# Four pairs of weight-word buffers and a separate half bank for one product in five sigmoid-gated head pairs of a hybrid attention block

## The chip, the cores and the metric

The kernel runs on one core of a Trainium2 chip. The metric is the device time of one execution in microseconds (us). Three runs of the kernel before gave 827.22, 828.13 and 829.1 us; the median is 828.13 us.

## What is computed

The reference is one decoder block on 512 tokens of width 2048: a normalisation, one large projection, two groups of attention heads, a gate on each head, an output projection, a residual and a final normalisation. Cut to what matters here:

```python
h = _rmsnorm(x, norm_g[l])
proj = h @ w_in[l]
(qa, kca, vca, ksa, vsa, kwa, vwa, za, ga, qb, kb, vb, zb) = jnp.split(proj, offsets, axis=-1)
...
y_a = o_a.reshape(B, S, WIDTH_A) * jax.nn.silu(za)
qb = _rope(_heads(qb, N_HEADS_B, HEAD_DIM_B))...
o_b = _banded_attention(qb, _rope(kb), vb, WIN_B, sink=sinks)
y_b = o_b.reshape(B, S, WIDTH_B) * jax.nn.silu(zb)
x = x + jnp.concatenate([y_a, y_b], axis=-1) @ w_out[l]
return _rmsnorm(x, final_g)
```

The change lies in the second group (`qb`, `zb`, `o_b`): 16 heads of 64 columns, handled as eight pairs of heads, each with 128 query columns and 128 gate columns to project.

## The kernel before, in words

Every float32 operand of a product is held as two words, a high word (`hi`, a rounded copy) and a low word (`lo`, the rest), and a product is three matmuls per block: high by high, high by low, low by high (`mm3`, lines 126 to 129, so the three lines L127, L128, L129 of the profile). For weights, ScalarE (ACT) makes the high word from the loaded block `raw` (tile `whi`, L643) and VectorE (DVE) subtracts it from `raw` to make the low word (`wlo`, L644); both are 128x1024. A pair `whi`, `wlo` is called words here. `words` (line 86) takes them from the pool `wp`, which has three buffers of each.

One head pair is projected by `pair(h)` (lines 689 to 770). The query and the gate columns together are a 2 by 2 block product, done with seven products instead of eight (the Winograd form of Strassen's scheme). Each has 8 blocks, so 24 matmuls of 128x256. Their names in the code and in this text are 22, p, 21, 12, w, u and q. Two PSUM banks hold them: `pa` and `pb`, from the pool `psp` (tile `pj`), which has two buffers; each bank has a left half H0 and a right half H1 of 256 columns.

- 22 goes to `pb` H0; ACT copies it, negated, to the tile `dd` (L732). 21 is added on top in the same place; ACT copies the sum to the right half of `zr` (L738).
- p goes to `pa` H0; DVE adds it to `dd` (L703, the helper `plus`). 12 is added on top in the same place; ACT copies the sum p+12 to the left half of the tile `t1` (`qv` in the code, L747).
- w goes to `pa` H1, and DVE adds it to `dd`. That is the last reader of `pa`.
- u goes to `pb` H1, q is added on top, and DVE adds them into the query and the gate.

Since `psp` has two buffers, the bank of `pa` becomes the `pb` of the next pair, so product 22 of pair h+1 can start when the last reader of `pa` of pair h is done. From h = 10 on (`wide`) a fifth load (`sm`, the sum of two quarters, added by an accumulating DMA that GpSimd issues, L699) takes the place of one addition on DVE.

The attention of the head pair before runs as jobs between these matmuls: scores (`spb`, L900 and L901, 16 matmuls), a masked maximum on DVE (`ttb`, L904), exponentials and scalings on ACT (L912, L918), transposes (`tp`, L930), words of the probabilities (`ph` on ACT L535, `pl` on DVE L536), products with the values (`opb`, L936, L937, L942), and a sum of two halves (`ob`: ACT L949, then DVE L950).

The order of the instructions on each engine is not written out by hand. A scheduler orders them when the program is built, by dependencies, by when buffers come free, and by times that it assumes; then each engine runs its list strictly in order. So a change in buffers reorders everything behind it. Loads go by the queue of SyncE (SP).

Pairs are counted here by h, 8 to 14; the third to the seventh pair of the group are 10 to 14. After pair 14 comes `plain(15, 0)`, the query columns of the last head pair as a plain product, whose first matmul takes the place of the next pair's 22.

Of the kernel before, what the change touches and what calls it, by code (L numbers as in the profile page):

```python
# [10 lines left out]
F32 = mybir.dt.float32  # L11
F32R = mybir.dt.float32r
AF = mybir.ActivationFunctionType
ALU = mybir.AluOpType
# [3 lines left out]
P = 128  # L18
S = 512
# [16 lines left out]
def hybrid_block(ctx, tc, xT, xtm, w0, w1s, w2s, wz, wq, wkb, wo0, wos, cw1, cw2, cpos, rope, tabs, sinks, gT, fg, out):  # L36
    nc = tc.nc
    pe, act, dve, pool = nc.tensor, nc.scalar, nc.vector, nc.gpsimd

    def sb(name, bufs=1, side=None):  # L40
        return tc.tile_pool(name=name, bufs=bufs, side=side)
# [40 lines left out]
    def raw():  # L82
        raws[0] += 1
        return weights(f"raw{raws[0] % 3}")

    def words(place):
        return [wp.tile([P, 1088], F32R, name=nm, tag=nm)[:, place:place + 1024] for nm in ("whi", "wlo")]

    def load_unit(src, width, rawp=None, opening=False, place=EVEN):
# [192 lines left out]
    H0, H1 = slice(0, 256), slice(256, 512)  # L282
# [246 lines left out]
    wk = wks.enter_context(sb("wk", bufs=2))  # L529
# [128 lines left out]
    def unit(raw):  # L658
        hi, lo = words(STILL)
        split(hi, lo, raw)  # L660
        return hi, lo
# [6 lines left out]
    def prod(bank, u, op, new, hooks=None):  # L668
        for m in range(8):
            cs = slice(m * P, m * P + P)  # L670
            ah, al = xf[op, m]
            mm3(bank, u[0][:, cs], u[1][:, cs], ah, al, new and m == 0, m == 7, not new)
            if m == 3:
                behind_mm((hooks or {}).get(op, ()))

    def swap_x(source):
        for part in range(2):
            ms = slice(4 * part, 4 * part + 4)
            for e in range(2):
                nc.sync.dma_start(even[e][:, ms], source[e, :, ms])  # L680
# [8 lines left out]
    def pair(h, early=(), hooks=None):  # L689
        src = wq[h - FIRST]  # L690
        early = list(early)
        wide = h > 9

        def load(tag, quarter, other=None):
            if early:
                return early.pop(0)
            t = load_quarter(src, tag, quarter)
            if other is not None:
                pool.dma_start(t, src[other], accum_op=ALU.add)  # L699
            return t  # L700

        def plus(out, a, b, op=ALU.add):
            return dve.tensor_tensor(out=out, in0=a, in1=b, op=op).ins  # L703

        if wide:
            c1, c2, c5, c3, c4 = tags
            tags[:] = c4, c1, c2, c3, c5
        else:
            c1, c2, c4, c3 = tags
            tags[:] = (c4, c1, c3, c2) if h < 9 else (c4, c1, "raw4", c3, c2)  # L710
        pa, pb = [psp.tile([P, S], F32, name="pj", tag="pj") for e in range(2)]

        qv = wk.tile([P, S], F32, name="t1", tag="t1", bufs=1)
        zr = wk.tile([P, S], F32, name="zr", tag="xr", bufs=1)
        d, jj = qv[:, H1], zr[:, H0]
        if wide:
            d = wb.tile([P, 256], F32, name="dd", tag="dd")
        x1 = load(c1, 3)
        u0 = unit(x1)
        x2 = load(c2, 0)  # L720
        u3 = unit(x2)
        if wide:
            sm = load(c5, 0, 2)
        else:
            sm = x2
            x4 = load(c4, 2)
            with ExitStack() as behind:
                if "jj" in last:
                    behind.enter_context(tc.issue_after(last["jj"]))
                plus(x2, x2, x4)  # L730
        prod(pb[:, H0], u0, "22", True, hooks)
        act.activation(d, pb[:, H0], AF.Copy, scale=-1.0)  # L732
        x3 = load(c3, 1)
        prod(pa[:, H0], u3, "p", True, hooks)
        plus(d, d, pa[:, H0])
        u2 = unit(x3)
        prod(pb[:, H0], u2, "21", False, hooks)
        act.activation(zr[:, H1], pb[:, H0], AF.Copy)  # L738
        plus(jj, d, zr[:, H1])
        u4 = unit(sm)  # L740
        if wide:
            x4 = load(c4, 2, 3)
        else:
            plus(x4, x4, x1)
        plus(sm, sm, x1)
        prod(pa[:, H0], u4, "12", False, hooks)
        act.activation(qv[:, H0], pa[:, H0], AF.Copy)  # L747
        plus(jj, jj, qv[:, H0], ALU.subtract)
        u1 = unit(x4)
        prod(pa[:, H1], u1, "w", True, hooks)  # L750
        plus(d, d, pa[:, H1])
        u5 = unit(sm)
        plus(sm, sm, x3)
        prod(pb[:, H1], u5, "u", True, hooks)
        plus(qv[:, H1], d, pb[:, H1])
        t2 = wk.tile([P, S], F32, name="t2", tag="t2", bufs=1)
        for a, b in ((0, 64), (64, 0)):
            dve.tensor_tensor(out=t2[a:a + 64], in0=qv[b:b + 64], in1=sinA[b:b + 64], op=ALU.mult)
        dve.tensor_tensor(out=qv, in0=qv, in1=cosA, op=ALU.mult)
        (pool if h < 8 else dve).tensor_tensor(out=qv, in0=qv, in1=t2, op=ALU.add)  # L760
        qq = q_split(qv) if h < 8 else qb_split(qv)
        u6 = unit(sm)
        prod(pb[:, H1], u6, "q", False, hooks)
        plus(jj, jj, pb[:, H1])
        behind_mm((hooks or {}).get("end", ()))
        last["jj"] = plus(zr, zr, rstdb, ALU.mult)
        st = wk.tile([P, S], F32, name="st", tag="st")
        act.activation(st, zr, AF.Tanh, scale=0.5)
        dve.scalar_tensor_tensor(out=st, in0=st, scalar=1.0, in1=zr, op0=ALU.add, op1=ALU.mult)
        return qq, st  # L770

    def plain(h, e, hooks=None):
        ps = psp.tile([P, S], F32, name="pj", tag="pj")
# [74 lines left out]
    wb = wbs.enter_context(sb("wb"))  # L848
# [4 lines left out]
    vb3 = wb.tile([P, P], F32, name="vb3")  # L853
    wb.tile([P, 3, 2, 2], F32, name="sums", tag="sums", bufs=2)
    wb.tile([P, 2, 256], F32, name="ttb", tag="ttb", bufs=4)
    wb.tile([P, S], F32, name="ob", tag="ob")
    nc.sync.dma_start(sk[:, 0, :], sinks)
    pool.tensor_scalar(sk[:, 1, :], sk[:, 0, :], -1.0, None, op0=ALU.mult)
    nc.sync.dma_start(cosB, ropeb[0])
# [22 lines left out]
    def attention(i, q2):  # L882
# [60 lines left out]

        def end():
            op = box["op"]
            ob = wb.tile([P, S], F32, name="ob", tag="ob")
            for v in range(2):
                hs = slice(v * 64, v * 64 + 64)
                act.activation(ob[hs], op[64:128, v, :], AF.Copy)  # L949
                dve.tensor_tensor(out=ob[hs], in0=op[0:64, v, :], in1=ob[hs], op=ALU.add)  # L950
            finish(8 + i, ob, box["st"])
# [6 lines left out]
    for i in range(7):  # L958
        hooks = {}
        if held:  # L960
            j, end, _ = held
            hooks = {"12": [j["s0"]], "w": [j["s1"]], "u": [j["k0"]], "q": [j["k2"], j["k3"]], "end": [j["k1"], end]}
        q2, st = pair(8 + i, (), hooks)
        if i == 0:
            back_b(0)
        if i == 2:
            back_b(1)
        held = attention(i, q2)
        held[2]["st"] = st
    swap_x(xd)  # L970
    for m in range(4):
        y_tile(m)
# [192 lines left out]
    for n in range(1, 4):  # L1165
# [55 lines left out]
        def plus(out, a, b, op=ALU.add):  # L1221
            dve.tensor_tensor(out=out, in0=a, in1=b, op=op)
# [12 lines left out]
        if n < 3:  # L1235
# [3 lines left out]
            jj = scratch()  # L1239
# [33 lines left out]
        else:  # L1273
# [64 lines left out]
            u1 = [pair()]  # L1338
# [121 lines left out]
```

## Time and profile before

| | |
|---|---|
| median of three runs | 828.13 us |
| the profiled execution, its own time | 826.69 us |
| its span, first to last instruction | 824.9 us |
| outside the span | 1.79 us |
| granted TensorE clock | 0.999 |
| pairs 10 to 14, about | 484 to 612 us of the span |

Times in the views are microseconds from the span's start. PE is TensorE, PEld its weight load. In a timeline row stand the start, the duration, the engine, the line, the output and inputs, and in brackets the idle time of that engine before it with what ended it. Names are without buffer numbers, so `pj` is `pa` or `pb` of any pair. A PE row of a 128x256 matmul lasts 0.28 us though the next starts about 0.12 us later, since matmuls overlap.

### The profile page before, as it was taken

The numbers are of one execution on the slowest core, as the hardware profiler recorded it, in microseconds if no ns is written. First come the engines' busy times: TensorE is split into PE (matmuls) and PEld (weight loads), VectorE is DVE, ScalarE is ACT, GpSimd is POOL, SyncE is SP. The second block draws the span as 40 slices with busy tenths as digits, with TensorE's granted clock in tenths as the row PEclk, the third lists the DMA queues.
The fourth block names the chain that finished last, engine by engine and source line by source line (L and its number), as shares of the span: only waits on it lengthen the run. The fifth ranks groups of instructions, "written<-read, shape, count | busy, mean of one in ns | idle before, by whom it ended". The sixth has DMA issues, their size and how long they took to land.

```text
span 824.9 us, 15435 instructions
## 1 busy us (share of the span) xinstructions
PE 797.2 (97%) x5782; PEld 750.0 (91%) x5782; DVE 685.4 (83%) x1271; ACT 529.4 (64%) x1103; POOL 76.4 (9%) x69
## 2 busy tenths in 40 slices
PE   9999999999999999999999989999999999999996
PEld 8788898988999999999999989989888788999996
DVE  7869786865898989998898789989977588977895
ACT  6734456662677867868776568766866776553545
POOL 4500002012011011011010000000000000000000
PEclk9999999999999999999999999999999999999999
DMA  9655886899712314412321685656595336597835
GB/s 320 206 200 166 290 301 195 272 333 353 223 52 66 104 40 141 154 51 79 116 78 63 195 206 135 186 145 166 139 314 183 91 102 218 138 302 181 259 79 204
DMA packets 60954, 145.29 MB, mean 176 GB/s; under 512 B 6352, under 2 KB 19920, under 8 KB 60880
## 3 DMA queue, kind: packets, MB, share of 16 engines
q1 hardware_dynamic: 57424, 132.26, 48.7%
q0 software_dynamic: 3168, 11.54, 8.1%
q8 instruction: 45, 0.74, 0.4%
q10 hardware_dynamic: 288, 0.52, 0.2%
q14 instruction: 29, 0.24, 0.1%
HBM read 121.65 MB, written 20.55 MB: 172 GB/s over the span
## 4 chain that ended last, share of the span: by engine, by line
PE 75%; DVE 9%; ACT 6%; DMA 5%; issue 3%; POOL 1%; SPq 0%; DVEq 0%; ACTq 0%
PE pj L127 13%; PE pj L129 13%; PE pj L128 13%; PE oa L128 4%; PE oa L129 4%; PE oa L127 4%; PE bank L129 4%; PE bank L127 4%; PE bank L128 3%; PE sp L567 3%; DVE wlo L644 2%; DMA raw<-wq 2%; ACT whi L643 1%; DVE raw L703 1%; DMA xr<-xT 1%
## 5 line engine op out<-in xcount | busy, mean ns | idle before, releaser
L127 PE MATMUL pj<-xh,whi 128*128 128x256 f32 (+1 forms) x560 | 170.7, 305 | 8.7 <-DVE sums L907 2.6
L129 PE MATMUL pj<-xh,wlo 128*128 128x256 f32 (+1 forms) x560 | 170.1, 304 | 1.7 <-DVE wlo L644 1.7
L128 PE MATMUL pj<-xl,whi 128*128 128x256 f32 (+1 forms) x560 | 168.8, 301 | 0.0
L643 ACT ACTIVATE whi<-raw 128x1024 fp32r<-128x1024 f32 x98 | 103.0, 1054 | 55.3 <-PE pj L128 33.2
L644 DVE TENSOR_TENSOR wlo<-raw,whi 128x1024 fp32r<-128x1024 f32 x98 | 121.4, 1242 | 12.7 <-ACT whi L643 12.3
L127 PEld LDWEIGHTS pj<-xh,whi 128*128 128x128 f32 x560 | 105.4, 188 | 15.8 <-ACT whi L643 3.0
L129 PEld LDWEIGHTS pj<-xh,wlo 128*128 128x128 f32 x560 | 105.6, 189 | 7.0 <-DVE wlo L644 2.5
L128 PEld LDWEIGHTS pj<-xl,whi 128*128 128x128 f32 x560 | 105.4, 188 | 4.2
L97 DVE TENSOR_TENSOR wlo<-raw,whi 128x512 fp32r<-128x512 f32 (+2 forms) x74 | 81.3, 1104 | 33.5 <-ACT whi L96 33.0
L96 ACT ACTIVATE whi<-raw 128x1024 fp32r<-128x1024 f32 (+1 forms) x73 | 65.5, 901 | 53.1 <-PE pj L128 17.3
L127 PE MATMUL pj<-pu,whi 128*128 128x256 f32 x224 | 64.2, 287 | 2.9 <-DVE sums L908 1.5
L129 PE MATMUL pj<-pu,wlo 128*128 128x256 f32 x224 | 63.2, 282 | 0.5 <-DVE wlo L644 0.5
L128 PE MATMUL pj<-pu,whi 128*128 128x256 f32 x224 | 63.3, 283 | 0.0
L703 DVE TENSOR_TENSOR raw<-raw 128x1024 f32<-128x1024 f32 x46 | 59.1, 1285 | 0.2
L128 PE MATMUL oa<-wlo,xh 128*128 128x256 f32 (+1 forms) x168 | 50.9, 303 | 0.7 <-DVE wlo L1008 0.7
L127 PE MATMUL oa<-whi,xh 128*128 128x256 f32 (+1 forms) x168 | 50.4, 303 | 1.0 <-DVE sums L904 1.0
L129 PE MATMUL oa<-whi,xl 128*128 128x256 f32 (+1 forms) x168 | 50.3, 302 | 0.0
L127 PEld LDWEIGHTS pj<-pu,whi 128*128 128x128 f32 x224 | 42.3, 189 | 4.2 <-issue 1.6
L129 PEld LDWEIGHTS pj<-pu,wlo 128*128 128x128 f32 x224 | 42.3, 189 | 1.0 <-DVE wlo L644 0.9
L128 PEld LDWEIGHTS pj<-pu,whi 128*128 128x128 f32 x224 | 42.2, 188 | 0.0
L536 DVE TENSOR_TENSOR pl<-tp,ph 128x512 fp32r<-128x512 f32 x56 | 37.7, 683 | 4.9 <-ACT ph L535 4.8
L535 ACT ACTIVATE ph<-tp 128x512 fp32r<-128x512 f32 x56 | 32.1, 588 | 12.4 <-PE tp L930 8.4
(372 smaller groups left out, 2325.6 us busy)
## 6 DMA issues: line engine op xcount, KB each, us to landing
raw<-wq SPq DMA_DIRECT2D x65, 512.0 KB, 4.1
raw<-cw SPq DMA_DIRECT2D x16, 512.0 KB, 5.2
raw<-wos SPq DMA_DIRECT2D x15, 512.0 KB, 5.0
raw<-wq POOLq DMA_DIRECT2D x10, 512.0 KB, 5.5
rw<-wos SPq DMA_DIRECT2D x10, 512.0 KB, 5.2
xr<-xT SPq DMA_DIRECT2D x16, 256.0 KB, 5.1
raw<-w SPq DMA_DIRECT2D x8, 512.0 KB, 4.4
fd<-ft SPq DMA_DIRECT2D x4, 1024.0 KB, 6.0
```

The costliest lines, as they stand in the source:

```text
L96: last["hi"] = act.activation(hi[:, :width], rw[:, :width], AF.Copy).ins
L97: last["lo"] = dve.tensor_tensor(out=lo[:, :width], in0=rw[:, :width], in1=hi[:, :width].bitcast(F32), op=ALU.subtract).ins
L127: pe.matmul(ps, ah, bh, start=first, stop=False, skip_group_check=go_on)
L128: pe.matmul(ps, ah, bl, start=False, stop=False, skip_group_check=go_on)
L129: recent["mm"] = pe.matmul(ps, al, bh, start=False, stop=last, skip_group_check=go_on).ins
L535: act.activation(ph, tp, AF.Copy)
L536: dve.tensor_tensor(out=pl, in0=tp, in1=ph.bitcast(F32), op=ALU.subtract)
L567: pe.matmul(sp[:, a:b], qq[:, qs], kk[0][:, ko:ko + b - a], start=pi == 0, stop=pi == 2)
L643: act.activation(hi, src, AF.Copy)
L644: last["lo"] = dve.tensor_tensor(out=lo, in0=src, in1=hi.bitcast(F32), op=ALU.subtract).ins
L703: return dve.tensor_tensor(out=out, in0=a, in1=b, op=op).ins
```

## The change

- From h = 10 on, a pool `w4` holds one more pair of word buffers, and every fourth call of `words` takes it. The pool is closed behind the last pair.
- From h = 10 on (`own`), product 12 does not go on top of p. ACT copies p alone (the copy L747 of before now reads p), 12 starts new in `pa` H1, and DVE takes it from there into the gate (`jj`) and onto the copy of p. Product w goes to `pa` H0. DVE adds p to `dd` from the copy in SBUF. That is one DVE operation of 128x256 more for each pair.
- To make room, `dd` takes the place of `pcr`, which the first group used, and `ob` shares the buffers of `pl`.

```diff
+    fourth = {"of": 0, "on": False}
     def words(place):
+        if fourth["on"]:
+            fourth["of"] += 1
+            if fourth["of"] % 4 == 0:
+                return [fourth["pool"].tile([P, 1024], F32R, name=nm, tag=nm) for nm in ("whi4", "wlo4")]
         return [wp.tile([P, 1088], F32R, name=nm, tag=nm)[:, place:place + 1024] for nm in ("whi", "wlo")]
...
         wide = h > 9
+        if h == 10:
+            fourth["pool"] = w4s.enter_context(sb("w4"))
+            fourth["pool"].tile([P, 48], F32, name="space")
+            fourth["on"] = True
...
-            d = wb.tile([P, 256], F32, name="dd", tag="dd")
+            d = wk.tile([P, 256], F32, name="dd", tag="pcr", bufs=1)
...
         prod(pa[:, H0], u3, "p", True, hooks)
-        plus(d, d, pa[:, H0])
+        own = wide
+        if own:
+            act.activation(qv[:, H0], pa[:, H0], AF.Copy)
+        else:
+            plus(d, d, pa[:, H0])
...
-        prod(pa[:, H0], u4, "12", False, hooks)
-        act.activation(qv[:, H0], pa[:, H0], AF.Copy)
-        plus(jj, jj, qv[:, H0], ALU.subtract)
+        if own:
+            prod(pa[:, H1], u4, "12", True, hooks)
+            plus(d, d, qv[:, H0])
+        else:
+            prod(pa[:, H0], u4, "12", False, hooks)
+            act.activation(qv[:, H0], pa[:, H0], AF.Copy)
+            plus(jj, jj, qv[:, H0], ALU.subtract)
         u1 = unit(x4)
-        prod(pa[:, H1], u1, "w", True, hooks)
-        plus(d, d, pa[:, H1])
+        if own:
+            plus(jj, jj, pa[:, H1], ALU.subtract)
+            plus(qv[:, H0], qv[:, H0], pa[:, H1])
+        w = pa[:, H0 if own else H1]
+        prod(w, u1, "w", True, hooks)
         u5 = unit(sm)
+        plus(d, d, w)
...
-            ob = wb.tile([P, S], F32, name="ob", tag="ob")
+            ob = wk.tile([P, S], F32, name="ob", tag="pl")
...
+    fourth["on"] = False
+    w4s.close()
```

Lines of the changed kernel are numbered higher: L644 of before is L650, L643 is L649, L703 is L713, L732 is L742, L738 is L752, L904 is L927, L950 is L973; L747 is the copy of p.

What the scheduler makes of it is shown at three places. The first is on ACT in pair 12, around the copy L747. Before, `whi_6764` is the high word for q of pair 12, `ttb_6603` and `ttb_6611` are probabilities of the head pair before, `t1_6482` is the copy:

```order
L643 ACTIVATE whi_6764<-raw_6497 128x1024 [waits DVE_49,PE_49]
L912 ACTIVATE ttb_6603,sums_6602<-ttb_6603,sums_6602 128x128 [waits DVE_49]
L949 ACTIVATE ob_6469<-opb_6365 64x512 [waits PE_49]
L912 ACTIVATE ttb_6603,sums_6602<-ttb_6603,sums_6602 128x128
L909 ACTIVATE sums_6602<-sums_6602 128x4 [waits DVE_49]
L912 ACTIVATE ttb_6611,sums_6602<-ttb_6611,sums_6602 128x256 x2
L747 ACTIVATE t1_6482<-pj_6480 128x256 [waits PE_49]
```

In the changed kernel the same copy, now of p, stands behind the high word for u (`whi4_6710`, in the fourth buffer, which p of the same pair held before):

```order
L941 ACTIVATE ttb_6311<-ttb_6311,sums_6310 128x256 [waits Activation_49]
L941 ACTIVATE ttb_6319<-ttb_6319,sums_6310 128x256 [waits Activation_49] x2
L790 ACTIVATE st_6482<-zr_6130 128x512 [waits DMAHW0_49,DVE_49]
L649 ACTIVATE whi4_6710<-raw_6502 128x1024 [waits PE_49]
L747 ACTIVATE t1_6487<-pj_6485 128x256 [waits PE_49,Activation_49]
L541 ACTIVATE ph_6433<-tp_6428 128x512 [waits PE_49]
```

The copy has moved from behind product 12 to behind product p, and five softmax instructions no longer stand ahead of it.

The second place is on DVE at the end of pair 13, ahead of the addition of w to `dd`, which frees the bank for product 22 of pair 14. Before (`spb_7029` are scores, `wlo_7202` the low word for 22 of pair 14, `pj_6837` is `pa`):

```order
L904 ISA ttb_7020,sums_7019<-spb_7021,tab_66 128x256
L904 ISA sums_7019 128x1
L644 TENSOR_TENSOR wlo_7202<-raw_7199,whi_7201 128x1024 [waits DMAHW1_49,Activation_49]
L914 TENSOR_TENSOR sums_6959<-sums_6959 128x4 [waits Activation_49]
L904 ISA ttb_7028,sums_7019<-spb_7029,tab_66 128x256 [waits PE_49]
L904 ISA sums_7019 128x1
L904 ISA ttb_7028,sums_7019<-spb_7029,tab_66 128x256
L904 ISA sums_7019 128x1
L703 TENSOR_TENSOR dd_6841<-dd_6841,pj_6837 128x256 [waits PE_49]
```

In the changed kernel (`wlo_7215` is the low word for p of pair 14, `ob_6832` the sum of two halves of the head pair before, `pj_6843` is `pa`):

```order
L927 ISA ttb_7035,sums_7026<-spb_7036,tab_66 128x256
L927 ISA sums_7026 128x1
L650 TENSOR_TENSOR wlo_7215<-raw_7212,whi_7214 128x1024 [waits DMAHW4_49,Activation_49]
L973 TENSOR_TENSOR ob_6832<-opb_6728,ob_6832 64x512 [waits Activation_49]
L937 TENSOR_TENSOR sums_6965<-sums_6965 128x4 [waits Activation_49]
L930 TENSOR_TENSOR sums_7026<-sums_7026,sk_5155 128x4 [waits DVE_49]
L713 TENSOR_TENSOR dd_6847<-dd_6847,pj_6843 128x256 [waits PE_49]
```

One low word stands among the maxima before and behind them now, and an `ob` and one more small operation have come ahead of the addition.

The third place is on ACT at the end of pair 11. In the changed kernel `whi4_6498`, the high word for p of pair 12, takes the fourth buffer, which w of pair 11 holds until its end, and the probabilities' word `ph_6376` is behind it; on PE its product with the values stands ahead of 22 of pair 12:

```order
L941 ACTIVATE ttb_6250<-ttb_6250,sums_6249 128x128 [waits Activation_49]
L941 ACTIVATE ttb_6258<-ttb_6258,sums_6249 128x256 [waits Activation_49] x2
L649 ACTIVATE whi4_6498<-raw_6496 128x1024 [waits DMAHW5_49,PE_49]
L541 ACTIVATE ph_6376<-tp_6371 128x512 [waits PE_49]
L935 ACTIVATE ttb_6311,sums_6310<-ttb_6311,sums_6310 128x256 [waits DVE_49]
```

Before, no product with the values stands between w of pair 11 and 22 of pair 12 on PE.

More of the change, by code (lines that the diff above doesn't have):

```diff
@@ L770, in pair @@
         return qq, st
+    w4s = ExitStack()
     def plain(h, e, hooks=None):
@@ L855, in hybrid_block @@
     wb.tile([P, 2, 256], F32, name="ttb", tag="ttb", bufs=4)
-    wb.tile([P, S], F32, name="ob", tag="ob")
     nc.sync.dma_start(sk[:, 0, :], sinks)
```

## The prediction

> **What bounds the kernel now.** The page first, for the busy shares.
>
> ```profile
> PE 797.2 (97%) x5782; PEld 750.0 (91%) x5782; DVE 685.4 (83%) x1271; ACT 529.4 (64%) x1103; POOL 76.4 (9%) x69
> ```
>
> TensorE bounds the kernel, so only what shortens or lengthens its gaps counts. Next the view by windows: pairs 10 to 14 as a whole, and one pair alone (pair 13).
>
> ```profile
> 484.60:612.00 127.40, 120.43 (x999) 116.38 (x1000) 114.24 (x248) 93.79 (x212) 6.10 (x7) 1.00 0.63 171
> ...
> 561.40:588.20 26.80, 25.49 (x217) 25.01 (x217) 24.69 (x55) 19.30 (x46) 1.73 (x2) 1.00 0.60 153
> ```
>
> In each row the length comes first, then PE, its weight load, DVE, ACT, POOL. PE is idle for 127.40 − 120.43 = 7.0 us of the five pairs: this is what there is to gain by the records. DVE is idle for 13.2 us, and for 2.1 us only in pair 13: it comes close behind PE. The same stretch by waits, of PE and then of ACT:
>
> ```profile
> PE pj L127 <- DVE sums L907: 2.6, 2, 1.3
> PE pj L127 <- ACT t L747: 1.9, 2, 1.0
> PE pj L127 <- ACT dd L732: 1.4, 1, 1.4
> PE pj L127 <- DVE dd L703: 1.3, 2, 0.9
> PE pj L127 <- ACT whi L643: 0.8, 2, 0.5
> PE pj L129 <- DVE wlo L644: 0.2, 1, 0.2
> ...
> ACT whi L643 <- PE pj L128: 11.6, 7, 4.2
> ```
>
> ACT stands 11.6 us before high words whose buffer PE still reads. The timeline gives PE's waits with their places, and ACT's around the copy L747 of pair 12.
>
> ```profile
> 502.57 0.39 PE L129 MATMUL pj<-xh,wlo 128*128 128x256 f32 x1 [0.24 <-DVE wlo L644]
> 528.91 0.36 PE L127 MATMUL pj<-xh,whi 128*128 128x256 f32 x1 [1.31 <-DVE sums L907]
> 542.23 0.38 PE L127 MATMUL pj<-pu,whi 128*128 128x256 f32 x1 [0.34 <-ACT whi L643]
> 548.00 1.06 ACT L643 ACTIVATE whi<-raw 128x1024 fp32r<-128x1024 f32 x1 [4.20 <-PE pj L128]
> 551.55 0.38 ACT L747 ACTIVATE t<-pj 128x256 f32<-128x256 f32 x1
> 551.99 0.39 PE L127 MATMUL pj<-xh,whi 128*128 128x256 f32 x1 [0.96 <-ACT t L747]
> 557.35 0.38 PE L127 MATMUL pj<-xh,whi 128*128 128x256 f32 x1 [0.87 <-DVE dd L703]
> 583.58 0.36 PE L127 MATMUL pj<-xh,whi 128*128 128x256 f32 x1 [1.31 <-DVE sums L907]
> 597.59 0.38 PE L127 MATMUL pj<-pu,whi 128*128 128x256 f32 x1 [0.47 <-ACT whi L643]
> 606.90 0.39 PE L127 MATMUL pj<-xh,whi 128*128 128x256 f32 x1 [0.95 <-ACT t L747]
> 611.80 0.50 PE L127 MATMUL pj<-xh,whi 128*128 128x512 f32 x1 [0.42 <-DVE dd L703]
> ```
>
> ACT's rows tell how two things hang together. A high word waited 4.20 us for its buffer, until 548.00. Behind it stood the softmax work and then the copy L747, which could start only at 551.55, although product 12 was long done; and PE's product w began at 551.99, behind the copy. Between w and the copy nothing is shared but the PSUM bank: the copy reads the left half, w writes the right one. So in this program one half waits for the other.
>
> The gaps are of three kinds. At pair ends (528.91, 557.35, 583.58, 611.80) 22 of the next pair waits for DVE's last addition of w to `dd` (where the row names `sums L907`, that addition stands just ahead of it on DVE): 1.31 + 0.87 + 1.31 + 0.42 = 3.91. Before w behind L747: 0.96 + 0.95 = 1.91. For words: 0.24 + 0.34 + 0.47 = 1.05.
>
> **The change part by part.** (a) *Product w.* The copy L747 goes from behind 12 to behind p, so the two waits before w go: −1.91. In their place w waits for two DVE operations on product 12, but product u stands between 12 and w on PE. What u covers is read from these rows, with 24 matmuls of 128x256 from the first to the last:
>
> ```profile
> 505.07 0.28 PE L127 MATMUL pj<-VH,whi 128*128 128x256 f32 x1
> ...
> 507.79 0.28 PE L129 MATMUL pj<-xh,wlo 128*128 128x256 f32 x1
> ```
>
> That is 2.72 us. Two DVE operations on 128x256 take 2 x 0.34 (one starts 0.34 behind the other: the fourth and fifth row of the next fence). So 0 is lost as long as DVE isn't 2 us late when 12 ends. If it is, the first new wait stands here; behind it on DVE a low word (`wlo_6851` in pair 12) is queued, and a late low word stops PE as well. That is the second rival.
>
> (b) *Words.* The fourth pair of buffers lets words be made one product earlier. The three word waits go: −1.05. The bound below nothing is in the weight loads, by line:
>
> ```profile
> L127 PEld LDWEIGHTS pj<-xh,whi 128*128 128x128 f32 x154 | 29.0, 188 | 9.2 <-ACT whi L643 3.0 <-ACT t L747 2.3 <-DVE dd L703 1.8
> ...
> L127 PEld LDWEIGHTS pj<-pu,whi 128*128 128x128 f32 x72 | 13.6, 188 | 1.3 <-ACT whi L643 1.2
> ```
>
> Weight loads stood 3.0 + 1.2 = 4.2 us for high words, where the matmul rows have 0.34 + 0.47 = 0.81. The next matmul can cover such a stand only in part. So (b) lies between 0 (new waits of the same sort elsewhere) and −1.05 − 3.4 = −4.4. I take −1.05, the recorded idle time, since PE's own rows are what adds up to the span.
>
> (c) *Pair ends.* The scheduler's new order puts other work ahead of the addition of w to `dd`. At the end of pair 13 the DVE rows of before are:
>
> ```profile
> 575.88 0.68 DVE L950 TENSOR_TENSOR ob<-opb,ob 64x512 f32<-64x512 f32 x1
> 576.48 0.41 DVE L703 TENSOR_TENSOR zr<-zr,t 128x256 f32<-128x256 f32 x1
> 576.82 0.15 DVE L907 TENSOR_TENSOR sums<-sums,sk 128x4 f32<-128x4 f32 x1
> ...
> 580.43 0.42 DVE L904 CUSTOM_DVE_ANT_0 ttb<-spb,tab 128x256 f32<-128x256 f32 x1 [0.45 <-PE spb L901]
> ...
> 581.12 1.22 DVE L644 TENSOR_TENSOR wlo<-raw,whi 128x1024 fp32r<-128x1024 f32 x1
> 582.26 0.15 DVE L914 TENSOR_TENSOR sums<-sums 128x4 f32<-128x4 f32 x1
> 582.33 0.42 DVE L904 CUSTOM_DVE_ANT_0 ttb<-spb,tab 128x256 f32<-128x256 f32 x1
> ...
> 583.02 0.42 DVE L703 TENSOR_TENSOR dd<-dd,pj 128x256 f32<-128x256 f32 x1
> ```
>
> By starts, two maxima take 581.12 − 580.43 = 0.69, the low word 1.14, a small operation 0.07, an `ob` 576.48 − 575.88 = 0.60. From the first maximum to the end of the addition: 583.02 + 0.42 − 580.43 = 3.01. In the new order the same stretch holds four maxima (1.38), a low word (1.14), an `ob` (0.60), two small operations (0.14) and the addition (0.42): 3.68. The maxima start when PE has made the scores, as before, so 22 of pair 14 waits 1.31 + 0.67 = 2.0 (+0.7).
>
> The other ends go the same way. PE's side is read from these rows: from the first to the last 20 matmuls, 2.36 us, 0.118 for one; four transposes 0.60 with the end of the last, which at 0.28 for one makes a step of 0.32 / 3 = 0.11. The mean durations are ACT's.
>
> ```profile
> 578.34 0.28 PE L127 MATMUL pj<-xh,whi 128*128 128x256 f32 x1
> ...
> 580.70 0.28 PE L127 MATMUL pj<-xh,whi 128*128 128x256 f32 x1
> ...
> 542.57 0.60 PE L930 MATMUL tp<-ident,ttb 128*128 128x128 f32 x4
> ...
> L643 ACT ACTIVATE whi<-raw 128x1024 fp32r<-128x1024 f32 x32 | 33.6, 1054 | 16.1 <-PE pj L128 11.6 <-DVE raw L703 2.3 <-DMA raw<-wq 0.9
> L535 ACT ACTIVATE ph<-tp 128x512 fp32r<-128x512 f32 x16 | 9.4, 590 | 2.5 <-PE tp L930 2.4
> L747 ACT ACTIVATE t<-pj 128x256 f32<-128x256 f32 x5 | 1.9, 384 | 0.8 <-PE pj L129 0.7
> ```
>
> - 14 to the plain product: the same DVE chain, 2.0 for 0.42: +1.6.
> - 12 to 13: behind the last matmul of u come a high word 1.05, its low word 1.14, two `ob` 1.20, four maxima 1.38, the addition 0.42: 5.2. Against it PE has 35 matmuls (w, 8 for scores, 3 with values) and four transposes: 35 x 0.118 + 0.43 = 4.6. A wait of 0.6 for 0.87: −0.3.
> - 11 to 12: here ACT sets it. `whi4_6498` takes the buffer that w of pair 11 held, so behind the end of w come 1.05 for it and 0.59 for `ph_6376`, whose product with the values stands on PE ahead of 22. Against that, four transposes 0.43: 1.2, and 1.31 before: −0.1.
> - 10 to 11: DVE has four maxima, a low word, three small ones and the addition, 1.38 + 1.14 + 0.2 + 0.42 = 3.1; PE has 19 matmuls, 2.2. Before, nothing was waited for: +0.9.
>
> Sum: 0.7 + 1.6 − 0.3 − 0.1 + 0.9 = +2.8. It lies between −3.9 (all four recorded end waits gone, if ACT and DVE are ahead by then) and +4.8 (one more `ob`, 0.60, ahead at three ends).
>
> (d) *12 behind the copy of p.* Product 12 now starts fresh in the other half, and by the bank it must wait until ACT has copied p. At pair 12, `whi4_6710` can start only when p has released its buffer, and the copy is behind it: 1.05 + 0.38, against six transposes of 0.11 on PE: 0.8, of which I take 0.7, a choice between that and the copy alone less its cover. In pairs 10 and 11 the copy alone stands there, 0.38, partly covered: 0.3 each; in 13 and 14 products with values and transposes lie between: 0. Sum +1.3, between 0 (PE has other work at each of the five) and 0.8 + 4 x 0.38 = 2.3 (none).
>
> [...]
>
> (e) *One more DVE operation for each pair*: 5 x 0.34 = 1.7, against 13.2 of idle time: 0, and 1.7 if the idle time lies in the wrong places.
>
> (f) *The tail.* The output products start with a wait:
>
> ```profile
> 654.12 0.47 PE L127 MATMUL oa<-whi,xh 128*128 128x512 f32 x1 [0.96 <-DVE sums L904]
> ```
>
> In the new order six more matmuls with values stand behind the last scores on PE ahead of the first `oa`, about 6 x 0.118 and their transposes: −0.9, between −0.96 and 0. Shared buffers (`ob` with `pl`, `dd` for `pcr`) add no wait in front of PE that I find: 0.
>
> Sum: −1.91 − 1.05 + 2.8 + 1.3 − 0.9 = +0.2. The profiled execution took 826.69 us (span 824.9), the median of three is 828.13, 1.44 above. So 826.9 for its like, **828.4** for the median.
>
> **The rivals.** R1, *faster: the words were worth more than PE's idle rows say.* For it: ACT's 11.6 us for buffers, and the 4.2 us of the weight loads beside 0.81 of the matmuls. With ACT a product ahead, low words and maxima come earlier too, and the pair ends shrink. Against it: DVE, not ACT, is last at the ends. The price: the whole of 3.4 more off the sum, +0.2 − 3.4 = −3.2, so 823.5 for the profiled execution and 824.9 for the median.
>
> R2, *slower: DVE becomes late.* For it: pair 13 had 2.1 us of DVE idle, the new operation takes 0.34 of it, and `ob` and low words move together ahead of `dd`. Product w then waits for its two DVE operations, which are queued behind low words and maxima. It decides from the point where DVE is more than 2.72 − 0.68 = 2.0 us late when 12 ends. A delay of one low word, one `ob` and three maxima, 1.14 + 0.60 + 1.04 = 2.8, is 0.8 over that; in all five pairs 5 x 0.8 = +4.0, so 828.4 + 4.0 = 832.4. Against it: 13.2 us idle over all.
>
> R3, *the change does little*: gaps go from w to 12 and from words to pair ends and come out even. That is my forecast itself.
>
> **How the numbers follow.** A measurement of this kernel can tell about 0.2%, 1.66 us, from no change: 826.47 to 829.79. The forecast, terms near their chosen values, has 0.37. R1 has 0.35, as the words are the larger half of the change and ACT's wait for them is the longest row. R2 has 0.28. So faster 0.35, same 0.37, slower 0.28. The range leaves out the ends: low, 823.6, is R1 with (d) gone too (824.9 − 1.3), high is R2, 832.4. That holds about 8 times in 10, as the outer parts of (b), (c) and (e) go on beyond both. The forecast alone would be 826.5 to 829.8.
>
> **What would show it.** In the profile after: no wait of w for ACT (a); the rows <-`whi` and <-`wlo` of PE near 0 between 484 and 612 us, and ACT's wait for PE at high words well under 11.6 (b); at the starts of 22 waits of 0.9, 1.2, 0.6, 2.0 and 2.0 us in the order of time, that name DVE, or at the second `ph` (c); a wait of 0.3 to 0.7 before 12 of pairs 10 to 12 that names L747 (d); no 0.96 before the first `oa` (f). R1 is shown by pair ends no longer than before and a stretch from pair 10 to 14 shorter by over 2 us; R2 by PE waiting for L713 before w and DVE busy over 95% there. I am wrong altogether if most of the difference lies outside 484 to 660 us.

## The result and the profile after

The changed kernel is slower. Its first four executions have a median of 837.1 us (831.86 to 840.03) beside 827.67 for the kernel before, a ratio of 1.010 with a 95% interval of 1.0053 to 1.0146. Timed again in eight executions it has 833.29 us beside 828.48 for before, ratio 1.0065 (1.0043 to 1.0087). All twelve together have a median of 833.4. The predicted 828.4 is missed, and 832.4, the upper end, is passed by both medians. The executions of the changed kernel spread over 8.7 us; their granted clock lies between 0.989 and 0.996, that of before at 0.997 in the mean of 31.

The profiled execution is one of the long ones, 839.89 us. Its page shows PE less busy in share, with a longer span.

```profile
span 838.1 us, 15420 instructions
...
PE 800.0 (95%) x5782; PEld 752.0 (90%) x5782; DVE 685.9 (82%) x1276; ACT 530.3 (63%) x1103; POOL 77.3 (9%) x69
```

From the span's start to product 21 of pair 10, the row whose 1.4 us wait for ACT stands in both kernels, it took 485.72 us (484.60 before; both times stand 0.04 us ahead of the row's own start). From there to the first product of plain(15, 0) it took 135.48 us, where before had 127.20, and from the plain product to the end 216.9, where before had 213.1. So of the 13.2 us in these two profiles 8.3 lie in pairs 10 to 14, 3.8 behind them, and 1.1 ahead of the change. The two places are two stories.

**Pairs 10 to 14.** PE's waits of 0.2 us and more there, picked from the timeline; the last row is the output products, far behind:

```profile
489.64 0.39 PE L133 MATMUL pj<-xh,whi 128*128 128x256 f32 x1 [0.87 <-ACT t L747]
504.96 0.39 PE L133 MATMUL pj<-xh,whi 128*128 128x256 f32 x1 [1.56 <-DVE dd L713]
513.48 0.39 PE L133 MATMUL pj<-xh,whi 128*128 128x256 f32 x1 [2.24 <-ACT dd L742]
522.27 0.39 PE L959 MATMUL opb<-ph,VB 128*128 128x256 f32 x1 [0.23 <-ACT ph L541]
536.80 0.39 PE L959 MATMUL opb<-ph,VB 128*128 128x256 f32 x1 [1.21 <-ACT ph L541]
550.08 0.39 PE L133 MATMUL pj<-xh,whi 128*128 128x256 f32 x1 [0.64 <-ACT t L747]
564.04 0.39 PE L133 MATMUL pj<-xh,whi 128*128 128x256 f32 x1 [0.91 <-DVE dd L713]
580.54 0.35 PE L923 MATMUL spb<-VH,qs 128*128 128x256 f32 x1 [0.53 <-DMA qs<-qlo]
592.15 0.45 PE L133 MATMUL pj<-xh,whi 128*128 128x256 f32 x1 [2.21 <-DVE dd L713]
621.20 0.47 PE L133 MATMUL pj<-xh,whi 128*128 128x512 f32 x1 [2.22 <-DVE dd L713]
...
710.45 0.38 PE L133 MATMUL oa<-whi,xh 128*128 128x256 f32 x1 [2.68 <-ACT whi L1032]
```

The waits for words and for the copy behind product 12 are gone. In their place stand the five pair ends: 1.56, 1.21 (the one that names `ph`), 0.91, 2.21 and 2.22, together 8.11 against 3.91 before. DVE at the fourth of them, from the timeline:

```profile
588.79 0.42 DVE L927 CUSTOM_DVE_ANT_0 ttb<-spb,tab 128x256 f32<-128x256 f32 x1
...
589.13 0.42 DVE L927 CUSTOM_DVE_ANT_0 ttb<-spb,tab 128x256 f32<-128x256 f32 x1
...
589.48 1.22 DVE L650 TENSOR_TENSOR wlo<-raw,whi 128x1024 fp32r<-128x1024 f32 x1
590.73 0.68 DVE L973 TENSOR_TENSOR ob<-opb,ob 64x512 f32<-64x512 f32 x1
591.44 0.16 DVE L937 TENSOR_TENSOR sums<-sums 128x4 f32<-128x4 f32 x1
591.52 0.16 DVE L930 TENSOR_TENSOR sums<-sums,sk 128x4 f32<-128x4 f32 x1
591.59 0.41 DVE L713 TENSOR_TENSOR dd<-dd,pj 128x256 f32<-128x256 f32 x1
```

The last matmul of w had started at 589.66. The low word and `ob` were still ahead of the one addition for which PE stood.

**Half clock.** The view by windows shows what the prediction had no row for: the granted clock (the third column from the end) behind the gap that ended at 513.48.

```profile
513.00:514.00 1.00, 0.52 (x3) 0.52 (x4) 0.94 (x1) 0.98 (x4) 0.00 (x0) 0.88 0.95 270
514.00:515.00 1.00, 1.00 (x7) 1.00 (x6) 1.00 (x3) 1.00 (x2) 0.00 (x0) 0.50 0.22 82
515.00:516.00 1.00, 1.00 (x6) 1.00 (x6) 1.00 (x2) 1.00 (x3) 0.00 (x0) 0.50 0.77 147
516.00:517.00 1.00, 1.00 (x7) 1.00 (x6) 1.00 (x3) 1.00 (x4) 0.00 (x0) 0.50 0.75 291
517.00:518.00 1.00, 1.00 (x10) 1.00 (x9) 1.00 (x2) 0.91 (x3) 0.00 (x0) 0.92 0.21 86
```

PE is busy, but only 4 or 5 matmuls start in each microsecond from 514 to 517, where 8 or 9 did from 505 to 511 (the counts in brackets also hold matmuls still under way from the microsecond before). In the trace's clock records the stretch lasts 3.41 us. It lasts the same 3.41 us behind 592.15 and behind 710.45; behind 621.20, after a gap of the same 2.2 us, the clock stays at 1.00. Before had half clock only in its last 2.2 us, from about 822.8 on.

### The profile page after: what moved, and what is told of

It is laid out like the page before. It is cut to its first block, busy times and chain, and to the rows that moved or that the text cites. A ratio compares the mean times of both kernels' runs of the same rounds, so it can differ in the third digit from the quotient of the medians.

```text
span 838.1 us, 15420 instructions
## 1 busy us (share of the span) xinstructions
PE 800.0 (95%) x5782; PEld 752.0 (90%) x5782; DVE 685.9 (82%) x1276; ACT 530.3 (63%) x1103; POOL 77.3 (9%) x69
## 4 chain that ended last, share of the span: by engine, by line
PE 56%; DVE 18%; DMA 12%; ACT 6%; issue 5%; POOL 1%; SPq 1%; DVEq 0%; ACTq 0%; POOLq 0%
PE pj L133 10%; PE pj L135 10%; PE pj L134 10%; PE sp L573 3%; DMA raw<-wq 3%; DMA rw<-wos 3%; DVE wlo L650 3%; PE bank L135 2%; PE bank L133 2%; PE bank L134 2%; PE oa L133 2%; PE oa L134 2%; PE oa L135 2%; DMA ch<-wos 1%; DVE raw L713 1%
## 5 line engine op out<-in xcount | busy, mean ns | idle before, releaser
L133 PE MATMUL pj<-xh,whi 128*128 128x256 f32 (+1 forms) x560 | 172.7, 308 | 13.6 <-DVE dd L713 6.9
L134 PE MATMUL pj<-xl,whi 128*128 128x256 f32 (+1 forms) x560 | 170.9, 305 | 0.0
L649 ACT ACTIVATE whi<-raw 128x1024 fp32r<-128x1024 f32 x98 | 103.1, 1056 | 64.0 <-PE pj L134 29.0
L650 DVE TENSOR_TENSOR wlo<-raw,whi 128x1024 fp32r<-128x1024 f32 x98 | 121.3, 1241 | 16.2 <-ACT whi L649 15.8
L713 DVE TENSOR_TENSOR raw<-raw 128x1024 f32<-128x1024 f32 x46 | 59.0, 1283 | 0.2
L133 PEld LDWEIGHTS pj<-pu,whi 128*128 128x128 f32 x224 | 42.3, 189 | 2.8 <-ACT whi L649 1.3
L135 PEld LDWEIGHTS pj<-pu,wlo 128*128 128x128 f32 x224 | 42.3, 189 | 1.2 <-DVE wlo L650 0.9
L134 PEld LDWEIGHTS pj<-pu,whi 128*128 128x128 f32 x224 | 42.2, 189 | 0.0
L134 PE MATMUL bank<-wlo,xh 128*128 128x256 f32 (+1 forms) x128 | 40.0, 315 | 0.4 <-DVE wlo L103 0.3
```

Of the source, the lines that this page charges most:

```text
L133: pe.matmul(ps, ah, bh, start=first, stop=False, skip_group_check=go_on)
L134: pe.matmul(ps, ah, bl, start=False, stop=False, skip_group_check=go_on)
L135: recent["mm"] = pe.matmul(ps, al, bh, start=False, stop=last, skip_group_check=go_on).ins
L649: act.activation(hi, src, AF.Copy)
L650: last["lo"] = dve.tensor_tensor(out=lo, in0=src, in1=hi.bitcast(F32), op=ALU.subtract).ins
```

## The experiments

Theory A at the start: the time is lost to the long gaps, which come from the own half bank, and to the half clock behind them. Rival B: the fourth buffers alone. Rival C: the tiles that were moved to make room. The first three kernels take the change apart.

**The two parts alone.** In `only_fourth` the half bank is off, in `only_half` the fourth buffers:

```diff
-        own = wide
+        own = False          # only_fourth
...
-            fourth["on"] = True   # this line left out: only_half
```

> The changed kernel with product 12 on top of p again (the bank use of before), and the fourth pair of word buffers kept. Theory A (the slowdown comes from TensorE gaps of about 2.2 us at pair ends and elsewhere, each of which is followed by some 3.5 us at half the granted clock; these gaps come from the order of work that the own half bank brings): no gap over 2 us in pairs 10 to 14, granted clock 0.998 or more, ratio to before 0.995 to 1.003. Rival B (the fourth pair of buffers alone reorders the work and makes the long gaps): ratio 1.006 to 1.015, granted clock 0.990 to 0.996.

> The changed kernel without the fourth pair of word buffers: product 12 in a half of its own, ACT copies p alone, one more DVE operation for each pair. Theory A: the long gaps stay (at least two of over 2 us in pairs 10 to 14 and on to the first output product), granted clock 0.990 to 0.996, ratio 1.006 to 1.015. Rival B: no gap over 2 us, ratio 0.997 to 1.004.

Measured: 832.81 us for the fourth buffers, ratio 1.0062 (1.0038 to 1.0086), and 832.38 for the half bank, ratio 1.0072 (1.0045 to 1.010). Both are slow, so neither A nor B holds as put. `only_fourth` shows every sign that B gave for it: gaps of 2.54 and 2.05 us in pairs 10 to 14, and a mean granted clock of 0.993. The profile of `only_half` has one gap over 2 us there (2.21) and half clock only at its very end. The third kernel says why both are slow.

**Neither part.** `only_room` has both edits; of the change it keeps the new places of `dd` and `ob`, the addition of w written behind the words of u, and the pool `w4`, opened but with no words taken from it.

> Neither part: only the two tiles that were moved to make room (dd in the place of pcr, ob with pl), and the addition of w to dd written behind the low word of u. Its order on DVE at the pair ends is that of before. Theories A and B both: ratio 0.998 to 1.002. Rival C (the shared buffers of ob and pl, or the later place of the addition, cost the time): ratio above 1.004.

Measured: 831.46 us, ratio 1.0049 (1.0031 to 1.0067), with the order on DVE at the pair ends as in before. Rival C was right, against A and B. Its trace has one new gap of over 2 us, in the output products; ACT's row tells what the high word waited for:

```profile
702.47 1.06 ACT L1031 ACTIVATE whi<-rw 128x1024 fp32r<-128x1024 f32 x1 [3.58 <-DMA rw<-wos]
...
703.58 0.58 PE L133 MATMUL oa<-whi,xh 128*128 128x256 f32 x1 [2.99 <-ACT whi L1031]
```

From 702.64 on the clock is at half for 6.83 us. ACT there waited for a load, `rw<-wos`. On SyncE's queue the order of the output loads has changed: one load of a quarter (`raw_8578`) stands five loads ahead of where it stood, in front of `ch`, the two `xs` and the two `rw`. Built without being timed, the kernel before with `ob` alone moved has the same change on that queue and no other; with `dd` alone moved the queue is that of before. SyncE's rows in `only_room`, and then in `room_tail`, the next kernel, where the load stands as in before (there it is the first of the last row's two):

```profile
690.48 0.33 SPq L1200 DMA_DIRECT2D raw<-wos  x1
692.09 0.33 SPq L1019 DMA_DIRECT2D ch<-wos  x1
...
693.45 1.28 SPq L1200 DMA_DIRECT2D rw<-wos  x2
```

```profile
691.84 0.33 SPq L1019 DMA_DIRECT2D ch<-wos  x1
...
693.20 1.12 SPq L1200 DMA_DIRECT2D rw<-wos  x2
694.36 4.84 SPq L1200 DMA_DIRECT2D raw<-wos  x2
```

**The load put back.** Three kernels issue that load behind the two `rw` again; the changed kernel runs beside them.

```diff
         r22 = [load(rw(), 3, g) for g in range(2)]
+        behind = last["dma"]
...
-            r12 = [load(raw(), 1, g) for g in range(2)]
+            r12 = [load(raw(), 1, 0)]
+            with ExitStack() as st:
+                if n == 1:
+                    st.enter_context(tc.issue_after(behind))
+                r12.append(load(raw(), 1, 1))
```

> The kernel with the two moved tiles alone, and in the output products one load put back where the kernel before has it on SyncE's queue: the second of the two loads of quarter 1 behind the two loads of quarter 3 (rw). Theory A2 (moving the tiles cost its 3.7 us because this load stands one place too early on SyncE, waits there for its buffer, and holds back the two loads that the output product 22 needs): ratio 0.998 to 1.002, no TensorE gap over 1.5 us between 690 and 715 us, and no half clock there. Rival C2 (the shared buffers themselves, in the attention, cost the time): ratio stays at 1.003 to 1.007.

> The changed kernel itself, timed again beside the three that follow, so that all four share the runs of the kernel before. Both theories: ratio 1.006 to 1.014, 832.5 to 839 us, granted clock 0.990 to 0.997 in its executions.

> The changed kernel with that load put back. Theory A2: 3 to 5 us less than the changed kernel as it is, so 831.5 to 835 us, ratio 1.004 to 1.009; what is left is lost in pairs 10 to 14 (gaps of 22 at the pair ends, and half clock behind the longest). Rival C2: no change against the changed kernel, ratio 1.008 to 1.014.

> The fourth pair of word buffers, with product 12 on top of p as before, the moved tiles, and that load put back. Pairs 10 to the first output product took 170.24 us with the fourth buffers against 169.48 before (0.8 more, about 2 of it a stretch at half clock). Theory A2: 0.8 us more than before at most, ratio 0.997 to 1.003. Rival C2: ratio 1.004 to 1.009, as without the load put back.

Measured: `room_tail` 826.01 us, ratio 0.9983 (0.9963 to 1.0002), no different from before; `after_again` 833.29 (1.0065); `after_tail` 830.09, ratio 1.0037 (1.0016 to 1.0057); `fourth_tail` 830.37, ratio 1.0020 (1.0004 to 1.0036). So one load in another place is worth 831.46 − 826.01 = 5.5 us with the tiles alone, 3.2 in the changed kernel and 2.4 with the fourth buffers. Only the changed kernel's two forms were timed side by side; between the two timings of the others the kernel before itself moved by 0.7 us. `after_tail` came out 1.4 us under the 831.5 to 835 that was expected of it, but the saving is within the 3 to 5. In `room_tail` the gap is 2 us shorter, and no half clock follows it as it does in `only_room`; from the first output product to the end it took 171.7 us for 176.1:

```profile
701.40 0.39 PE L133 MATMUL oa<-whi,xh 128*128 128x256 f32 x1 [1.01 <-ACT whi L1031]
```

The mechanism was not quite the one expected. SyncE was not held up: the first `rw` was issued 693.45 − 656.21 = 37.2 us behind the first output product in `only_room` and 693.20 − 656.01 = 37.2 in `room_tail`. The loads landed later. The DMA view of 18 us around, of `only_room` and then of `room_tail` (last column: us from issue to landing):

```profile
xs<-xtm SPq DMA_DIRECT2D x2, 512.0 KB, 7.2
rw<-wos SPq DMA_DIRECT2D x2, 512.0 KB, 9.3
ch<-wos SPq DMA_DIRECT2D x1, 512.0 KB, 5.7
```

```profile
xs<-xtm SPq DMA_DIRECT2D x2, 512.0 KB, 5.5
rw<-wos SPq DMA_DIRECT2D x2, 512.0 KB, 8.4
ch<-wos SPq DMA_DIRECT2D x1, 512.0 KB, 3.8
```

One more transfer of 512 KB is under way among the five, and each lands 0.9 to 1.9 us later. The first `rw`, for whose high word PE waits, took 8.9 us for 7.0, and that is the difference of the two gaps.

**The half bank with the load put back.** The same line in `only_half`.

> Product 12 in a half of its own without the fourth pair of word buffers, the moved tiles, and the load of the output products put back. The moved tiles with the load put back took 826.0 us, the fourth buffers on top of that 830.4, both parts 830.1. Theory A3 (each part by itself lets the scheduler put other work ahead of what TensorE waits for, so the two losses don't add): 828 to 831 us. Rival: the half bank costs nothing by itself and the fourth buffers all of it: 825.5 to 827 us.

Measured: 831.14 us, ratio 1.0033 (1.0011 to 1.0054). Theory A3 holds, though this kernel is 0.1 us above A3's 828 to 831: 830.4 for the fourth buffers, 831.1 for the half bank, 830.1 for both, over 826.0 for neither. `only_half` has the load in the early place too; here putting it back gives 832.38 − 831.14 = 1.2 us, which is not clear of the noise of six and twelve executions. The losses don't add, since either part makes a new order, and each order has gaps of its own. In `fourth_tail` the long ones are these:

```profile
512.38 0.33 PE L953 MATMUL tp<-ident,ttb 128*128 128x128 f32 x1 [2.88 <-ACT ttb L941]
...
590.75 0.39 PE L133 MATMUL pj<-xh,whi 128*128 128x256 f32 x1 [2.05 <-DVE dd L713]
```

**Gaps made on purpose.** To the kernel before, operations are added behind the addition of w:

```diff
         plus(d, d, pa[:, H1])
+        for n in range({10: 4, 11: 1, 12: 3, 13: 2, 14: 7}.get(h, 0)):
+            dve.scalar_tensor_tensor(out=d, in0=pa[:, H1], scalar=0.0, in1=d, op0=ALU.mult, op1=ALU.add)
```

> The kernel before, with 4, 1, 3, 2 and 7 DVE operations of 128x256 behind the addition of w in pairs 10 to 14 (they add 0 times the product to dd, so that the values stay), which read the bank again and so hold back product 22 of the next pair: gaps of TensorE of about 1 to 3 us at the five pair ends. Theory A (a gap over some 2 us costs twice: itself, and about 3.5 us at half clock): granted clock 0.50 for 3 to 4 us behind each gap of over 2.2 us, and 1.00 behind each of under 1.6 us. Rival D (the lower clock in the changed kernel had another cause, such as the chip's load): the clock stays at 1.00 behind all five gaps, or falls without regard to them.

One execution, 840.27 us. The scheduler put the gaps partly elsewhere; these are the ones that tell, and behind them the windows that follow the first four:

```profile
481.12 0.35 PE L127 MATMUL pj<-pu,whi 128*128 128x256 f32 x1 [2.27 <-DVE sums L910]
506.22 0.36 PE L127 MATMUL pj<-xh,whi 128*128 128x256 f32 x1 [2.41 <-ACT ph L535]
562.99 0.58 PE L939 MATMUL opb<-pl,VB 128*128 128x256 f32 x1 [2.24 <-DVE pl L536]
592.94 0.33 PE L932 MATMUL tp<-ident,ttb 128*128 128x128 f32 x1 [1.81 <-ACT ttb L920]
...
622.11 0.33 PE L932 MATMUL tp<-ident,ttb 128*128 128x128 f32 x1 [1.81 <-ACT ttb L920]
...
625.25 0.58 PE L938 MATMUL opb<-ph,VB 128*128 128x256 f32 x1 [1.72 <-ACT ph L535]
```

```profile
482.00:484.00 2.00, 2.00 (x19) 2.00 (x18) 1.44 (x2) 2.00 (x9) 0.72 (x2) 1.00 0.53 53
506.00:508.00 2.00, 1.78 (x15) 1.81 (x16) 1.97 (x6) 2.00 (x5) 0.00 (x0) 1.00 0.98 190
563.00:565.00 2.00, 1.69 (x6) 1.39 (x7) 1.90 (x7) 1.96 (x8) 0.00 (x0) 0.50 0.76 119
...
593.00:595.00 2.00, 1.64 (x7) 1.34 (x8) 1.93 (x6) 2.00 (x8) 0.86 (x1) 0.55 0.33 70
```

Half clock comes behind gaps, so rival D falls; but the length alone doesn't decide, so A's rule in its sharp form falls too: 2.27 and 2.41 pass, 2.24 and 1.81 don't. The latter two have more idling close by (1.24 us ahead of the one, 0.36 and transposes behind the other). So has a fifth place: 1.81 and 1.72 us within 3.1 us, with half clock for 6.83 us from 623.92 on. That the idling close by decides is not shown; it is what these three have in common.

**Work in the gaps.** The changed kernel with the load put back, and matmuls with zero weights ahead of 22 of pair 14 and ahead of the plain product; what they add to u is zero.

```diff
+        ww = recent["mm"]          # the last matmul of w
...
         prod(pb[:, H1], u5, "u", True, hooks)
+        if h > 12:
+            with tc.issue_after(ww):
+                for n in range(14):
+                    pe.matmul(pb[:, H1], fourth["zero"], VB[:, 0].rearrange("p a b -> p (a b)"), start=False, stop=False, skip_group_check=True)
```

> The changed kernel with the load put back, and at the ends of pairs 13 and 14 fourteen matmuls with weights of zero on top of u (they add nothing to it) between the last matmul of w and product 22: about 1.65 us of TensorE work inside the two gaps of 2.2 us, with 22 no earlier than before. Theory A (behind a gap of about 2.2 us the clock falls to half in about every second case, each costing some 1.8 us): gaps of 0.4 to 0.8 us there, no half clock behind them, 0.5 to 2.5 us less than the 830.1 us without, mean granted clock 0.996 to 0.999. Rival D (the clock has another cause): half clock there as often as before, 830 to 831 us.

Measured: no half clock from pair 10 to the last products in its profile, and a mean granted clock of 0.9971 over twelve executions, where `after_tail` has 0.9954 over twelve. But 831.52 us, ratio 1.0038 (1.0020 to 1.0055): the 0.0017 of clock, 1.4 us of 830, doesn't show in the time. So the clock went A's way, and its gain is not shown. The comparison isn't clean either: another order came with the extra tile (the wait of 0.96 us before the first output product is back, which `after_tail` doesn't have), and the added matmuls fill 1.81 us of the gap at the end of pair 13 and leave 0.57.

**The addition ahead.** The low word for p of the next pair and the two `ob` are put behind the addition of w to `dd`, in the changed kernel and in the one with the fourth buffers alone, each with the load put back.

```diff
-        plus(d, d, w)
+        last["dw"] = plus(d, d, w)
...
-        u3 = unit(x2)
+        with ExitStack() as st:
+            if h > 10:
+                st.enter_context(tc.issue_after(last["dw"]))
+            u3 = unit(x2)
...
-                dve.tensor_tensor(out=ob[hs], in0=op[0:64, v, :], in1=ob[hs], op=ALU.add)
+                with tc.issue_after(last["dw"]):
+                    dve.tensor_tensor(out=ob[hs], in0=op[0:64, v, :], in1=ob[hs], op=ALU.add)
```

> The changed kernel with the load put back, and with an order on DVE: from pair 11 on the low word for p of the next pair, and in all pairs the sum ob, stand behind the addition of w to dd. Theory A: the gaps ahead of 22 at the ends of pairs 13 and 14 fall from 2.2 to 0.5 to 1.0 us, no half clock in pairs 10 to 14, 825 to 828 us. Rival E (DVE has no time to spare, and what is put behind is waited for at the next place): the gaps come back before other products, 829 to 832 us.

> The same order on DVE for the fourth buffers with product 12 on top of p, load put back (830.4 us without the order). Its two long gaps are 2.9 us before transposes in pair 11 (ACT late) and 2.05 us at the end of pair 13; the order only bears on the second. Theory A: that one falls under 1.2 us, the first stays with its half clock, 828 to 830 us. If the first goes too, 825 to 828 us. Rival E: 830 to 832 us.

Measured: `after_ends` 834.17 us, ratio 1.0062 (1.0040 to 1.0083). The gaps at the ends of pairs 13 and 14 are under 0.6 us, as A has it, but others have opened, with half clock behind both:

```profile
519.15 1.11 PE L956 MATMUL tp<-ident,ttb 128*128 128x128 f32 x4 [2.73 <-ACT pd L966]
535.54 0.35 PE L133 MATMUL pj<-xh,whi 128*128 128x256 f32 x1 [2.30 <-DVE dd L713]
```

So it is rival E here, and 2 us more than the 832 that E allowed. The first of these gaps comes from the edit by a long way: the second `ob` starts on DVE at 508.94 (507.60 in `after_tail`), the store of the block that holds it is issued at 512.43 and lands 5.68 us later, and ACT stands 4.27 us for that store before it can go on to the operations that PE waits for. A third stretch of half clock stands behind a wait of 2.13 us before p of pair 10 (480.44), where `after_tail` waits 1.80. With the fourth buffers alone the same edit gives 829.12 us, ratio 1.0013 (0.9994 to 1.0031): 1.3 us less than 830.4, not clear of it, and no different from before. There A was right in each sign: the gap at the end of pair 13 fell from 2.05 to 1.05, the long one of pair 11 (2.60) stayed with its half clock, and the time lies in A's 828 to 830. No version here beats the kernel before.

## Why the prediction was wrong, step by step

**Step (f) failed first**, in its last sentence: "Shared buffers (`ob` with `pl`, `dd` for `pcr`) add no wait in front of PE that I find: 0." I had looked for waits on the shared buffers. What `ob` set off was an order on SyncE's queue, in code that the diff doesn't touch; in the changed kernel its wait came 710.45 − 621.20 = 89 us behind the plain product. It cost 1.2 to 5.5 us in four pairs of kernels, and 3.2 in the changed kernel, of the 833.3 − 828.4 = 4.9 us by which the second timing missed the forecast. That was the prediction's own sign of being wrong altogether: most of the difference to before, 3.2 of 4.8 us by that timing, lies behind 660 us, though in the two profiles above 8.3 of 13.2 lie ahead of it. The −0.9 of the same step came in name only: the wait of 0.96 before the first output product is gone, but one of 0.80 for a load (`qs<-qlo`, at 635.92) has opened ahead of it, and the stretch from the plain product on is 42.2 us for 42.3.

**(a) and (b) were right** in their sums. No wait of w and none for words is left among the rows from 489.64 to 621.20. One sign of (b) failed: ACT still stands 10.0 us for PE at high words, for 11.6, and 10.5 us for DVE's sums of `raw` blocks, for 2.3. That 12 waits for the bank, as (d) has it, was right as well: 0.87 and 0.64 behind the copy of p.

**(c) had the right places and was too small.** Forecast, in order of time: 0.9, 1.2, 0.6, 2.0, 2.0, sum 6.7; measured 1.56, 1.21, 0.91, 2.21, 2.22, sum 8.1. So +4.2 in the place of +2.8. About half of the miss is the end of pair 10 (0.7). There 3.1 us of DVE work were set against 19 matmuls, and the sum leaves out that DVE itself stands 0.40 us for a high word of ACT in the middle of that work:

```profile
502.52 1.23 DVE L650 TENSOR_TENSOR wlo<-raw,whi 128x1024 fp32r<-128x1024 f32 x1 [0.40 <-ACT whi L649]
```

The upper end given for (c), +4.8, should be 2.8 + 3 x 0.60 = +4.6 by its own terms.

**(d) was about right** in the sum, by the changed kernel's trace: 0.87 + 0.64 = 1.5 for 1.3. That is partly luck: pair 11 has none for 0.3, and pair 10, forecast at 0.3, has 0.87 here, 1.40 in `after_again` and none over 0.2 in `after_tail`. Only the 0.64 of pair 12, forecast at 0.7, comes in all three. The low end of the range, 823.6, takes (d) as gone; none of the three shows that.

**Missing: 21 of pair 11.** It waits 2.24 us for ACT's `dd`, with this on ACT:

```profile
511.97 1.06 ACT L649 ACTIVATE whi<-raw 128x1024 fp32r<-128x1024 f32 x1 [2.97 <-DMA raw<-wq]
513.05 0.38 ACT L742 ACTIVATE dd<-pj 128x256 f32<-128x256 f32 x1
```

On PE 21 stands ahead of p in this pair now (513.48, p from 518.43); before had p first (509.27, 21 from 512.21), so the 24 matmuls of p no longer cover the copy of product 22. And on ACT a high word for a load that hadn't landed stood ahead of that copy: the head-of-line wait that L747 had before, at another place. In `after_again` and `after_tail` the same wait is 0.86 and 0.85, so part of it was that execution's transfers. Step (d) looked only at the copy that the diff moves, not at the other one on ACT.

**Missing: the clock.** Every gap was priced at its own length. The stretches at half clock cost more PE time: from pair 10 to the plain product PE is busy for

```profile
485.72:621.20 135.48, 122.83 (x994) 119.12 (x995) 114.05 (x251) 93.58 (x209) 6.10 (x7) 0.97 0.61 165
```

in the changed kernel with two such stretches, and in `after_tail`, the same instructions with none of them before the plain product, for

```profile
485.75:615.69 129.94, 119.88 (x994) 116.11 (x995) 113.84 (x251) 93.52 (x209) 6.12 (x7) 1.00 0.62 170
```

That is (122.83 − 119.88) / 2 = 1.5 us for each; `after_again`, with one, has 121.17. The 8.3 us of pairs 10 to 14 add up so: −1.91 and −1.05 as forecast, +4.2 at the pair ends, +1.5 before 12, +2.24 at 21 of pair 11, +0.8 for the rows at 522.27 and 580.54, and 122.83 − 120.24 = 2.6 more of busy PE than before. Those two stretches are not all of the time between 830 and 837 us, and with `after_warm` it stays open how much of the clock's loss reaches the end.

**The rivals.** R1 has nothing for it in the changed kernel: no stretch got shorter (from the plain product to the first output product 42.2 us, 42.3 before). R2 gave nearly the right time, 832.4, by a wrong way: w never waits for its two additions, so u covers them, as (a) says. DVE did become the one that PE waits for, but at the pair ends.

What is left of `after_tail` over `room_tail`, 4.1 us, with intervals of 0.2% on either side, is of the size of the recorded gaps (10.1 us in pairs 10 to 14 against 7.0 in before and 7.9 in `room_tail`, with 0.96 more in both of these before the first output product) and one or two stretches at half clock. It isn't settled further.

## What to carry to other kernels

Where a scheduler orders the work, moving one tile can reorder loads far behind the edit: compare each engine's whole list, DMA queues and the tail included, and time the edits that only make room by themselves. A wait removed on one engine is worth what the new order leaves of it (here 2.96 us went before w and for words, and 4.2 came at the pair ends); the operation that frees a bank should not stand behind filling work (2.21 and 2.22 us at the ends of pairs 13 and 14), yet putting it ahead by force may open gaps as long elsewhere (2.73 and 2.30 in `after_ends`). In these traces half clock followed 15 of the 24 idle stretches of TensorE of 2.0 to 3.3 us from 479 us on, and each of the two stretches at half clock in pairs 10 to 14 of the changed kernel cost 1.5 us of busy time: price a gap of that length at itself and a part of that.

## What the runs showed of the hardware that was not expected

Over all traces here, of sixteen gaps of 2.0 to 2.5 us from 479 us on, eight were followed by half clock, and of eight gaps of 2.5 to 3.3 us seven; the one that was not is the longest of all, 3.31 us in `after_again`. Away from the kernel's end each stretch lasts 3.41 us or twice that, 6.83. The changed kernel shows both sides with one order: of its gaps of 2.21 and 2.22 us the first is followed by half clock in two profiles and the second is not, and in the third (`after_tail`) it is the other way. So half clock followed a gap of about 2.2 us in half of the cases, and one of 1.81 us in two places of `gaps` with idle time close by. That one order runs both ways doesn't show as a wider spread of the times: side by side, the standard deviation is 2.0 us for the changed kernel (`after_again`) and 1.9 for before.
